# Five reordered operations at the seam of two sweeps in a hybrid encoder layer: a copy of masked scores, two low parts, one load and one gate

## The chip, the core and the metric

The kernel runs on one core of a Trainium2 chip. Its engines work side by side, each through its own queue in order: TensorE (PE, matrix products and transposes), VectorE (DVE), ScalarE (ACT), GpSimd (POOL), and SyncE (SP), which here only issues transfers. An instruction starts when those ahead of it on its engine have started and the semaphores it waits for have been raised; whatever stands behind a waiting instruction waits too. The metric is the device time of one execution in microseconds (us), as the median of several runs.

## What is computed

One encoder layer over 2048 tokens of width 1024: a gated linear attention in 4 heads (chunked, forward and backward scans) beside a latent attention in 4 heads (low-rank queries and keys/values, a shared rotary key, dense softmax), both gated, joined, projected and normalised.

```python
h = x @ w_in
(g_q, g_k, g_v, g_gate, g_lr_f, g_lr_b, m_cq, m_ckv, m_kr, m_gate) = jnp.split(h, idx, axis=-1)
# group A, per chunk and direction:
attn = jnp.where(mask, einsum('nbhtd,nbhsd->nbhts', q_dec, k_dec), 0.0)
o = einsum('nbhts,nbhsv->nbhtv', attn, vc) + einsum('bhtd,bhdv->bhtv', qd, state)
o_a = rms_norm(o_fwd + o_bwd, norm_g) * silu(g_gate)
# group B:
q = rms_norm(c_q, q_norm_g) @ w_uq
kv = rms_norm(c_kv, kv_norm_g) @ w_ukv
s = q_nope @ k_nope.T + rope(q_rope) @ rope(k_rope).T
o_b = softmax(s) @ v * silu(m_gate)
x = layer_norm(ALPHA * x + concat(o_a, o_b) @ w_out, ln_g, ln_b)
```

## The kernel before

**Precision.** Matrix operands in fp32 are carried as a high and a low part (`hi`, a copy into the matmul type, L378; `lo`, source minus high part, L384), and each product is three matmuls: high·high, high·low, low·high (`mm3`, L432 to L434). The high part is a copy on ACT; the low part is a subtraction on DVE or POOL.

**Stages.** There are 16 chunks of 128 tokens. The first sweep (`sweep_a`) goes through them from the last (15) to the first (0): input projections `ipa`, the gate product `ipg` and its silu (`gate_end`, tile `gs`, stored to `u_s`), the decayed queries and keys, the scores within a chunk `Ap`, the masked scores `At`, their product with the values `Op`, and the backward state. The gates of chunks 15 and 14 come behind it, with the loads and splits of the weights for what follows (`late_gates`). The second sweep (`sweep_c`) takes the chunks upwards, two to a step: projections `ipm` (448 columns: compressed queries `cq`, compressed keys/values `ckv`, the rotary key `kr`), gate products `pz`, the first group's output (`Ob`, then its norm and gate `og`), transposes `tm` of the compressed queries into `cqT` (high and low part), the rotary queries `pqr` and the absorbed queries `pq`. Then the softmax attention, with the output projection at its end.

**What sets the order.** In the second sweep a table of numbers sets it: every operation has a place per chunk of the pair, and all operations of all steps are sorted by step plus place; that is the order on each engine. The first step has a table of its own, `PLACE_C_FIRST`; its second entry is that of the odd chunk, chunk 1. The step's setup, `su_lset`, issues seven loads of small weights on SP. In the first sweep's last piece the code is in plain order, and `self.after(...)` around `gate_end(0, ...)` keeps the gate's instructions behind the named ones on the engines these run on.

**Names for the steps below.** In the last chunk of the first sweep, chunk 0, `At` is written twice: ACT copies half of `Ap` (L1071, PSUM to SBUF), then DVE overwrites it under a mask (L1073); PE needs it for `Op` (L1080). The gate of chunk 0 is three ACT passes over `gs` (L1582, L1584, L1586) and one product on DVE (L1588). In the second sweep `krf` (L1571) begins the rotary key on DVE, POOL completes it (L1400), ACT takes the high part `krs` and POOL the low part (L384, `krs<-krf,krs`). There is one `krf` buffer, so the next chunk's `krf` waits for that low part. `cqT_l` (L384 on DVE) is the low part of the compressed queries, which the third product of `pqr` reads (L434). `pq` takes the PSUM buffer that `Ob` of chunk 2 held, which is free when DVE has written `og` (L1554).

Of the kernel before, what the change touches and what calls it, by code (L numbers as in the profile page):

```python
# [12 lines left out]
AF = mybir.ActivationFunctionType  # L13
# [123 lines left out]
    cqTl=(0.758, 1.185),  # L137
# [51 lines left out]
    cqTl=(0.758, 1.284),  # L189
# [8 lines left out]
    krsl=(0.456, 1.044),  # L198
# [64 lines left out]
    ssm=(0.095, 0.913),  # L263
    rmd=(0.194, 0.9775),
    krf=(-0.407, 0.869),
    cqTl=(0.579, 1.316),
    ckvTl=(0.54, 1.33),
    qrf=(0.9795, 1.46),
    qrTl=(1.322, 1.703),
# [2 lines left out]
    Sf1=(-1.303, -0.0225),  # L272
    Sf2=(-0.613, -0.022),
    krfa=(-0.119, 0.94),
    krsl=(0.252, 1.09),
    vl=(0.627, 1.365),
    qrfa=(1.04, 1.476),
    lS=(-1.12, -1.093),
# [48 lines left out]
    cqTl=(0.598, 1.211),  # L327
# [8 lines left out]
    krsl=(0.395, 0.879),  # L336
# [30 lines left out]
class K:  # L367
# [272 lines left out]
    def sweep_a(self):  # L640
        tc, nc, ins, cp = self.tc, self.nc, self.ins, self.cp
        with ExitStack() as ctx:
# [61 lines left out]
            ch = self.ch = [dict(cst, c=NCH - 1 - i, i=i, lr=lrs[i % 2]) for i in range(NCH)]  # L704
# [48 lines left out]
            for t in ORDER_A.split():  # L753
                n, i = t.split(".")
# [22 lines left out]
            i = NCH - 1  # L777
# [6 lines left out]
                    run("kt", i)  # L784
            self.xlate.append(self.split_x(self.xab, self.xraw, NCH - 2, "xb", "dve", 2))
            run("intra", i)
            with self.after(ch[i]["Aset"]):
                self.gate_end(0, g1)
            run("state", i)
            run("av", i)  # L790
# [271 lines left out]
    def ga_intra(self, d):  # L1062

        nc, c = self.nc, d["c"]
        Ap = d["gp"].tile([P, 2, H, P], F32, tag="gp", name=f"Ap{c}")
        for h in range(H):
            for j, r in enumerate((slice(0, 64), slice(64, 128))):
                nc.tensor.matmul(Ap[:, j, h], d["kd"][r, h], d["qd"][r, h], start=True, stop=True)
        yield
        At = d["At"] = self.t512(d, "At")  # L1070
        nc.scalar.activation(At, Ap[:, 1], AF.Copy)  # L1071
        yield
        d["Aset"] = nc.vector.copy_predicated(At, d["mask"][:, None, :].to_broadcast([P, H, P]), Ap[:, 0]).ins  # L1073
        yield
# [139 lines left out]
    def su_lset(self):  # L1214
        nc, ins, w1 = self.nc, self.ins, self.w1
        self.gq = self.bc.tile([P, 2], F32, name="gq")
        self.gkv_b = w1.tile([P, H, P], F32, tag="oT", name="gkv_b", bufs=2)[:, 0]
        t1 = w1.tile([P, 2, 512], F32, tag="qa", name="wkr")
        self.wkT = t1[:, 0].rearrange("p (h l) -> p h l", h=H)
        self.wqr = t1[:, 1].rearrange("p (c d) -> p c d", c=2)  # L1220
        self.wqT = w1.tile([P, H, 256], F32, tag="gm", name="wqT")
        for t, n in ((self.gq, "gq_col"), (self.gkv_b, "gkv_bc"), (self.wqr, "wqr"), (self.wkT, "wkT"),
                     (self.wqT, "wqT"), (self.gkv_c, "gkv_col"), (self.gn_c, "gn_col")):
            nc.sync.dma_start(t, ins[n])
        self.wa = [None, None]

# [935 lines left out]
```

## Time and profile before

| | us |
|---|---|
| median of three runs (lowest, highest) | 1252.93 (1252.37, 1253.10) |
| the profiled execution, its own time | 1252.8 |
| its span, first to last instruction | 1251.0 |
| PE busy in the span | 1232.6 |
| DVE, ACT, POOL busy | 908.6, 732.1, 729.6 |
| mean granted TensorE clock | 0.999 |

The span is 1.8 us shorter than the execution's time, which also holds what lies around the instructions. PE is busy 99% of the span by modelled ends of pipelined matmuls, so what can be gained without removing work is the 18 us in which PE stands still, and these lie in few places. In a row of the timeline below stand the start, the duration, the engine, the line, the operation with output and inputs and their shapes, and in brackets how long the engine had stood idle before it and what released it.

### The profile page before, as it was taken

How to read it: one execution, taken by the hardware profiler on the slowest of the kernel's cores; microseconds unless marked ns; L12 is line 12 of the kernel's file. 1: busy time of each engine (PE TensorE's matmuls, PEld its weight loads, DVE VectorE, ACT ScalarE, POOL GpSimd, SP SyncE). 2: the span in 40 equal slices, each digit the busy share in tenths (PEclk: the TensorE clock that was granted, in tenths of full speed). 3: DMA queues.
4: the chain of work that ended last, by engine and by line, in shares of the span. 5: the costliest groups of instructions: out<-in, count | busy, mean ns of one | idle time of the engine just before them, and what ended most of it. 6: DMA issues, size and time to landing. Idle time of an engine off the chain costs nothing.

```text
span 1251.0 us, 18895 instructions
## 1 busy us (share of the span) xinstructions
PE 1232.6 (99%) x6464; PEld 1066.4 (85%) x6464; DVE 908.6 (73%) x1695; ACT 732.1 (59%) x1171; POOL 729.6 (58%) x445
## 2 busy tenths in 40 slices
PE   8999999999999999999999999999999999999997
PEld 7999999999888889897788888888888888888886
DVE  6636454544566776676999999899999998388775
ACT  7543434344565555545888888888888888411110
POOL 0132313232355555531798888889999999954650
PEclk9999999999999999999999999999999999999999
DMA  8225555555756888869543333313346310376652
GB/s 297 72 81 131 133 146 137 142 138 145 256 185 205 245 249 249 249 182 215 95 70 65 58 59 60 76 26 76 76 110 122 77 47 19 129 242 221 214 180 83
DMA packets 311568, 173.95 MB, mean 139 GB/s; under 512 B 212806, under 2 KB 264910, under 8 KB 311472
## 3 DMA queue, kind: packets, MB, share of 16 engines
q1 hardware_dynamic: 310352, 170.62, 50.9%
q0 software_dynamic: 672, 2.10, 0.4%
q8 instruction: 51, 0.84, 0.3%
q14 instruction: 45, 0.37, 0.1%
q10 hardware_dynamic: 448, 0.03, 0.0%
HBM read 113.93 MB, written 67.14 MB: 145 GB/s over the span
## 4 chain that ended last, share of the span: by engine, by line
PE 93%; ACT 2%; DVE 2%; DMA 2%; issue 1%; SPq 0%; POOL 0%; DVEq 0%; ACTq 0%; POOLq 0%
PE ipm L1366 5%; PE o L432 5%; PE o L434 5%; PE o L433 5%; PE ipa L432 5%; PE pS L1640 5%; PE pS L1636 5%; PE pS L1638 5%; PE pS L1637 5%; PE pS L1639 4%; PE ipa L434 4%; PE ipa L433 4%; PE po L433 3%; PE po L434 3%; PE po L432 3%; PE ipg L434 2%
## 5 line engine op out<-in xcount | busy, mean ns | idle before, releaser
L384 POOL TENSOR_TENSOR pl<-s,ph 128x1024 fp32r<-128x1024 f32 x128 | 306.9, 2417 | 47.6 <-ACT ph L378 43.9
L1645 ACT ACTIVATE s<-pS 128x1024 f32<-128x1024 f32 x128 | 131.5, 1028 | 54.8 <-PE pS L1640 49.8
L1658 DVE TENSOR_TENSOR rm<-pS,rm 128x512 f32<-128x512 f32 x210 | 144.7, 689 | 18.2 <-ACT s L1645 12.7
L1682 DVE TENSOR_TENSOR s<-s,mb 128x1024 f32<-128x1024 f32 x128 | 151.2, 1213 | 9.2 <-PE mb L1676 9.1
L378 ACT ACTIVATE ph<-s 128x1024 fp32r<-128x1024 f32 x128 | 134.9, 1056 | 15.6 <-PE o L434 15.0
L1686 ACT ACTIVATE s<-s 128x1024 f32<-128x1024 f32 x128 | 131.6, 1051 | 10.7 <-DVE s L1682 10.0
L432 PE MATMUL ipa<-wah,xah 128*128 128x384 f32 (+1 forms) x384 | 128.6, 335 | 5.0 <-ACT wah L378 5.0
L433 PE MATMUL ipa<-wal,xah 128*128 128x384 f32 (+1 forms) x384 | 124.4, 324 | 0.7 <-DVE wal L384 0.7
L434 PE MATMUL ipa<-wah,xal 128*128 128x384 f32 (+1 forms) x384 | 124.1, 323 | 0.0
L1105 POOL TENSOR_TENSOR Sb<-Sb,Us 64x512 f32<-64x512 f32 x15 | 19.9, 1325 | 170.2 <-DVE Us L1097 161.1
L1636 PE MATMUL pS<-qh,kvT 128*128 128x512 f32 x256 | 102.7, 401 | 0.8 <-DVE rm L1658 0.4
L432 PE MATMUL o<-ph,vh 128*128 128x512 f32 x256 | 101.1, 395 | 0.0
L1640 PE MATMUL pS<-rl,kvT 128*128 128x512 f32 x256 | 100.0, 391 | 0.6 <-DMA rl<-qr_s 0.6
L1638 PE MATMUL pS<-qh,kvT 128*128 128x512 f32 x256 | 100.0, 391 | 0.0
L1637 PE MATMUL pS<-ql,kvT 128*128 128x512 f32 x256 | 99.9, 390 | 0.0
L1639 PE MATMUL pS<-rh,kvT 128*128 128x512 f32 x256 | 99.8, 390 | 0.0
L434 PE MATMUL o<-ph,vl 128*128 128x512 f32 x256 | 99.7, 390 | 0.0
L433 PE MATMUL o<-pl,vh 128*128 128x512 f32 x256 | 99.7, 389 | 0.0
L1709 DVE TENSOR_TENSOR ap<-ap,s 128x512 f32<-128x512 f32 x120 | 82.9, 691 | 2.7 <-ACT s L1686 0.7
L432 PEld LDWEIGHTS ipa<-wah,xah 128*128 128x128 f32 x384 | 72.6, 189 | 8.3 <-ACT wah L378 5.4
L433 PEld LDWEIGHTS ipa<-wal,xah 128*128 128x128 f32 x384 | 72.8, 189 | 2.1 <-DVE wal L384 1.5
L1714 POOL TENSOR_TENSOR acc<-acc,s 128x1024 f32<-128x1024 f32 x30 | 72.6, 2420 | 1.1
(312 smaller groups left out, 3255.8 us busy)
## 6 DMA issues: line engine op xcount, KB each, us to landing
xcf<-xT_dram SPq DMA_DIRECT2D x16, 512.0 KB, 5.2
xr<-x_dram SPq DMA_DIRECT2D x16, 512.0 KB, 6.5
out_dram<-rr SPq DMA_DIRECT2D x32, 256.0 KB, 3.3
xaf<-xT_dram SPq DMA_DIRECT2D x14, 512.0 KB, 4.1
oib<-oi_s SPq DMA_DIRECT2D x16, 256.0 KB, 5.2
qdb<-qd_s SPq DMA_DIRECT2D x16, 256.0 KB, 3.3
SU<-su_s SPq DMA_DIRECT2D x16, 256.0 KB, 5.2
ub<-u_s SPq DMA_DIRECT2D x16, 256.0 KB, 4.0
```

What stands on the lines that cost most here:

```text
L378: return nc.scalar.activation(dst, src, AF.Copy).ins
L384: return e.tensor_tensor(dst, src, hi.bitcast(F32), ALU.subtract).ins
L432: mm(out, ah, bh, start=start, stop=False)
L433: mm(out, ah, bl, start=False, stop=False)
L434: mm(out, al, bh, start=False, stop=stop)
L1636: mm(ps[:, e], kh, qh, start=True, stop=False)
L1637: mm(ps[:, e], kh, ql, start=False, stop=False)
L1638: mm(ps[:, e], kl, qh, start=False, stop=False)
L1639: mm(ps[:, e], kr, rh, start=False, stop=False)
L1640: mm(ps[:, e], kr, rl, start=False, stop=True)
L1658: V.tensor_tensor(d["rm"], src[:, e], d["rm"], ALU.max)
L1682: V.tensor_tensor(s, s, d["mb"][:, None, :].to_broadcast([P, 2, QB]), ALU.subtract)
```

## The change

Four edits, no operation added or taken away. Two numbers of `PLACE_C_FIRST`, those of chunk 1: `cqTl` from 1.316 to 1.206 and `krsl` from 1.09 to 1.035. `gate_end(0, ...)` is kept behind the ACT copy of `At` too, and not only behind the masked overwrite on DVE. The load of `gkv_b` goes from second to last of the seven.

```diff
@@ PLACE_C_FIRST
-    cqTl=(0.579, 1.316),
+    cqTl=(0.579, 1.206),
-    krsl=(0.252, 1.09),
+    krsl=(0.252, 1.035),
@@ sweep_a
             run("intra", i)
-            with self.after(ch[i]["Aset"]):
+            with self.after(ch[i]["Acopy"], ch[i]["Aset"]):
                 self.gate_end(0, g1)
@@ ga_intra
-        nc.scalar.activation(At, Ap[:, 1], AF.Copy)
+        d["Acopy"] = nc.scalar.activation(At, Ap[:, 1], AF.Copy).ins
@@ su_lset
-        for t, n in ((self.gq, "gq_col"), (self.gkv_b, "gkv_bc"), (self.wqr, "wqr"), (self.wkT, "wkT"),
-                     (self.wqT, "wqT"), (self.gkv_c, "gkv_col"), (self.gn_c, "gn_col")):
+        for t, n in ((self.gq, "gq_col"), (self.wqr, "wqr"), (self.wkT, "wkT"), (self.wqT, "wqT"),
+                     (self.gkv_c, "gkv_col"), (self.gn_c, "gn_col"), (self.gkv_b, "gkv_bc")):
             nc.sync.dma_start(t, ins[n])
```

**First place: ACT at the end of the first sweep, before.** `xbh` is the high part of chunk 14's input, for its late gate, `gs` the gate of chunk 0, `At` the masked scores, `oi` the evacuation of `Op`.

```order
L378 ACTIVATE kt_3672<-kt_3667 128x512
L378 ACTIVATE xbh_3680<-xbf_3474 128x512 x2
L1582 ACTIVATE gs_3698<-ipg_3648 128x512
L1584 ACTIVATE gs_3698<-gs_3698 128x512
L1071 ACTIVATE At_3695<-Ap_3686 128x512
L1586 ACTIVATE gs_3698<-gs_3698 128x512
L1083 ACTIVATE oi_3720<-Op_3715 128x512
```

The same place of the changed kernel:

```order
L378 ACTIVATE kt_3672<-kt_3667 128x512
L378 ACTIVATE xbh_3680<-xbf_3474 128x512 x2
L1071 ACTIVATE At_3695<-Ap_3686 128x512
L1582 ACTIVATE gs_3698<-ipg_3648 128x512
L1584 ACTIVATE gs_3698<-gs_3698 128x512
L1586 ACTIVATE gs_3698<-gs_3698 128x512
L1083 ACTIVATE oi_3720<-Op_3715 128x512
```

The copy of `At` has moved past two of the gate's passes. With it the gate's product on DVE (L1588) goes behind the scaling of the state's update `Us` (L1097), and on POOL the store of `gs` goes behind those of `Us` and `oi`.

**Second place: DVE in the second sweep's first pair of chunks, where the rotary queries of chunk 0 are done, before.** `krf` and `rope` are the rotary key of chunk 2, `Ob` and `ss` the first group's output of chunk 2 and its norm, `cqT_l` the low part of chunk 1's queries.

```order
L1571 TENSOR_TENSOR krf_4283<-ipm_4188,cos 128x64
L1575 TENSOR_TENSOR rope_2_4284<-ipm_4188,sin 128x32 x2
L1534 TENSOR_TENSOR Ob_4271<-Ob_4271,oib_4096 128x512
L1421 STREAM_TRANSPOSE kvx_4289<-vh 128x128
L1421 STREAM_TRANSPOSE kvx_4289<-vl 128x128
L1421 STREAM_TRANSPOSE kvx_4289<-krs_4048 128x128
L1477 STREAM_TRANSPOSE qrx_4293<-qrf_4232 128x256
L1379 TENSOR_SCALAR ssm_4268<-ssm_4268 128x1 x2
L1543 TENSOR_REDUCE Ob_4271<-og_4305 128x4
L1544 TENSOR_SCALAR ss_4311<-Ob_4271 128x4
L384 TENSOR_TENSOR cqT_l_4102<-tm_4276,cqT_h_4101 128x2x128
L384 TENSOR_TENSOR qrT_4307<-qrx_4293,qrT_4307 128x256
```

DVE at the same place of the changed kernel:

```order
L384 TENSOR_TENSOR cqT_l_4102<-tm_4276,cqT_h_4101 128x2x128
L1571 TENSOR_TENSOR krf_4284<-ipm_4188,cos 128x64
L1575 TENSOR_TENSOR rope_2_4285<-ipm_4188,sin 128x32 x2
L1534 TENSOR_TENSOR Ob_4271<-Ob_4271,oib_4096 128x512
L1421 STREAM_TRANSPOSE kvx_4290<-vh 128x128
L1421 STREAM_TRANSPOSE kvx_4290<-vl 128x128
L1421 STREAM_TRANSPOSE kvx_4290<-krs_4048 128x128
L1477 STREAM_TRANSPOSE qrx_4294<-qrf_4232 128x256
L1379 TENSOR_SCALAR ssm_4268<-ssm_4268 128x1 x2
L1543 TENSOR_REDUCE Ob_4271<-og_4306 128x4
L1544 TENSOR_SCALAR ss_4312<-Ob_4271 128x4
L384 TENSOR_TENSOR qrT_4308<-qrx_4294,qrT_4308 128x256
```

`cqT_l` has moved past ten rows, to just ahead of `krf`.

**Third place: POOL beside it, before.** `krs` is the low part of chunk 1's rotary key, `qrf` the rotary queries of chunk 0, `xcl` the low part of chunk 3's input.

```order
L1400 TENSOR_TENSOR krf_4176<-krf_4176,rope_1_4177 128x64
L1473 TENSOR_TENSOR qrf_4232<-qrf_4232,rope_0_4233 128x256
L384 TENSOR_TENSOR krs_4243<-krf_4176,krs_4243 128x64
L384 TENSOR_TENSOR xcl<-xcf_4155,xch 128x8x128
L1511 TENSOR_TENSOR Sf_4280<-Sf_4071,cw 64x512
```

POOL at the same place of the changed kernel:

```order
L1400 TENSOR_TENSOR krf_4176<-krf_4176,rope_1_4177 128x64
L384 TENSOR_TENSOR krs_4243<-krf_4176,krs_4243 128x64
L1473 TENSOR_TENSOR qrf_4232<-qrf_4232,rope_0_4233 128x256
L384 TENSOR_TENSOR xcl<-xcf_4155,xch 128x8x128
L1511 TENSOR_TENSOR Sf_4280<-Sf_4071,cw 64x512
```

`krs` has moved past `qrf` and no longer stands behind what `qrf` waits for. On SP, `gkv_b` now follows `gn_c` and stands just ahead of the loads of the first group's stored states (`SU`); `gq` keeps its place and each of the other five loads moves up by one. PE's order is as it was.

## The prediction

> **What bounds the kernel now.** I read the page first for who sets the end, then the waits of PE, then the stretches by window, and last the timelines of all engines around each wait.
>
> ```profile
> span 1251.0 us, 18895 instructions
> PE 93%; ACT 2%; DVE 2%; DMA 2%; issue 1%; SPq 0%; POOL 0%; DVEq 0%; ACTq 0%; POOLq 0%
> PE pqr L434 <- DVE cqT_l L384: 1.1, 1, 1.1
> PE Op L1080 <- DVE At L1073: 0.6, 1, 0.6
> PE pq L432 <- DVE og L1554: 0.2, 1, 0.2
> 396.40:536.00 139.60, 139.60 (x780) 125.64 (x779) 97.33 (x333) 73.91 (x198) 77.52 (x82) 1.00 0.83 241
> ```
>
> The second line is the chain that ended last: 93% of it is PE. The next three are waits of PE between 325 and 410 us (total, times, longest). The last is a window (length, then busy time of PE, PEld, DVE, ACT, POOL, granted clock, DMA share, GB/s): PE is busy for all 139.60 us of the second sweep's middle. So PE sets the time, and an earlier start of that stretch moves everything behind it, as long as the helpers keep up. The edits bear on the three waits, which lie ahead of it.
>
> **First part: the copy of `At` ahead of the gate.**
>
> ```profile
> 332.83 1.16 PE L1068 MATMUL Ap<-qd,kd 64*128 64x128 f32 x16
> 335.15 0.40 PE L433 MATMUL ipg<-wgl,xbh 128*128 128x512 f32 x1
> 335.39 0.40 PE L434 MATMUL ipg<-wgh,xbl 128*128 128x512 f32 x1
> 336.36 1.16 PE L1080 MATMUL Op<-V,At 128*128 128x128 f32 x8 [0.58 <-DVE At L1073]
> 333.82 0.58 ACT L1582 ACTIVATE gs<-ipg 128x512 f32<-128x512 f32 x1
> 334.96 0.58 ACT L1071 ACTIVATE At<-Ap 128x512 f32<-128x512 f32 x1
> 333.42 1.29 DVE L384 TENSOR_TENSOR xbl<-xbf,xbh 128x512 fp32r<-128x512 f32 x2 [4.96 <-ACT xbh L378]
> 335.58 0.73 DVE L1073 COPY_PREDICATED At<-mask,Ap 128x512 f32<-128x512 int32 x1 [0.86 <-ACT At L1071]
> ```
>
> `Ap` ends at 332.83 + 1.16 = 333.99, and ACT is free for `At` from 333.82. So the copy starts at about 334.0 and ends at 334.6. DVE is busy with `xbl` until 333.42 + 1.29 = 334.71; the overwrite then runs from about 334.7 to 335.4, 0.9 us earlier. PE's product before `Op` starts at 335.39, and such products follow each other by 0.24 us (335.15 to 335.39), so `Op` could start at 335.63 and its operand is there by then. The gain is 336.36 − 335.63 = **0.73 us**; its floor is the listed idle time, 0.58, its ceiling the 0.9 by which `At` is earlier. What pays: the gate's passes end some 0.5 us later, at about 336.4, and the next ACT work (the evacuation of `Op`) can't start before `Op`'s new end, 336.8. That hides it; without this cover it would cost one pass, 0.58. The gate's product on DVE goes behind `Us`, and nobody but its store reads it soon.
>
> **Second part: the two low parts.**
>
> ```profile
> 380.65 0.47 DVE L1575 TENSOR_TENSOR rope<-pqr,sin 128x128 f32<-128x128 f32 x2
> 382.25 0.23 DVE L1571 TENSOR_TENSOR krf<-ipm,cos 128x64 f32<-128x64 f32 x1 [1.13 <-POOL krs L384]
> 385.01 0.41 DVE L384 TENSOR_TENSOR cqT_l<-tm,cqT_h 128x256 fp32r<-128x256 f32 x1
> 385.34 0.51 DVE L384 TENSOR_TENSOR qrT<-qrx,qrT 128x256 fp32r<-128x256 f32 x1
> 385.78 0.15 DVE L456 TENSOR_TENSOR rg_t<-Ob,ss 128x4 f32<-128x4 f32 x1
> 386.55 1.13 DVE L1554 SCALAR_TENSOR_TENSOR og<-Ob,rg_r,ub 128x128 f32<-128x128 f32 x4
> 381.20 0.74 POOL L1473 TENSOR_TENSOR qrf<-qrf,rope 128x256 f32<-128x256 f32 x1 [7.22 <-DVE rope L1575]
> 381.90 0.32 POOL L384 TENSOR_TENSOR krs<-krf,krs 128x64 fp32r<-128x64 f32 x1
> 382.18 2.40 POOL L384 TENSOR_TENSOR xcl<-xcf,xch 128x1024 fp32r<-128x1024 f32 x1
> 376.98 0.24 ACT L378 ACTIVATE krs<-krf 128x64 fp32r<-128x64 f32 x1
> 379.48 0.37 ACT L378 ACTIVATE cqT_h<-tm 128x256 fp32r<-128x256 f32 x1
> 385.37 0.18 ACT L446 ACTIVATE Ob<-rg_l 128x4 f32<-128x4 f32 x1
> 385.48 0.39 PE L434 MATMUL pqr<-wqr_h,cqT_l 128*128 128x256 f32 x1 [1.13 <-DVE cqT_l L384]
> 387.82 0.35 PE L432 MATMUL pq<-cqT_h,wabs_h 128*128 128x256 f32 x1 [0.19 <-DVE og L1554]
> ```
>
> Here DVE stands 1.13 us before `krf`, because POOL's `krs` is queued behind `qrf`, which itself waits 7.22 us for DVE's `rope`. ACT has the high part at 376.98 + 0.24 = 377.22, so moved ahead, `krs` fits into POOL's idle 7 us and is done by 377.6; without that cover it would cost its 0.32. DVE ends `rope` at 381.12. `cqT_l` comes next (its input is there at 379.48 + 0.37 = 379.85) and takes 385.34 − 385.01 = 0.33 from start to start, so `krf` starts at 381.45 in place of 382.25: 0.80 earlier. The same 0.33 falls away further down, ahead of `qrT`; but `rg_t` needs ACT's result, ready at 385.37 + 0.18 = 385.55 against a start of 385.78, so of it some 0.2 counts. `og` ends 1.0 earlier. PE alone would gain more: the wait before `pqr`'s third product (1.13) and that before `pq` (0.19), 1.32 together. But `pq` needs the buffer that `og` frees, so `og`'s **1.0 us** counts, and about 0.3 us of PE's stall moves from `pqr` to `pq`. Ceiling 1.32; floor 0.1, from the first rival. All times of this part shift along with the first part's gain, since its engines work off PE's results there.
>
> **Third part: the load.**
>
> ```profile
> SPq L1224 <- DMA u_s<-gs: 1.4, 1, 1.4
> 346.64 0.33 SPq L1224 DMA_DIRECT2D gn_c<-gn_col_dram  x1
> 347.45 0.80 SPq L1492 DMA_DIRECT2D SU<-su_s  x2
> gkv_b<-gkv_bc_dram SPq DMA_DIRECT2D x1, 64.0 KB, 4.0
> 337.40 0.57 POOL L916 DMA_DIRECT2D u_s<-gs  x1
> 353.95 0.52 POOL L1523 MEMSET SU<- 64x512 f32 x1
> 356.07 0.74 DVE L1255 SCALAR_TENSOR_TENSOR wabs<-pabs,gq,gkv_b 128x512 f32<-128x512 f32 x1
> 359.73 1.06 PE L1531 MATMUL Ob<-SU,qdb 128*128 128x128 f32 x8
> ```
>
> The first row is SP's own wait at `gkv_b`: its memory is free only when the store of `gs` has landed, 343.7, some 6.3 us after issue. The first part makes that store later: it is now behind two more issues of 0.57 each, so at about 338.5, and lands at about 344.8. At the end of the list `gkv_b`'s turn comes after `gn_c`, about 347.0, when the store is done. It lands 4.0 later, at 351, and `wabs` reads it at 356.07. The six loads ahead go earlier, `SU` hardly moves. I price this part at nothing; cover: 5 us for `wabs`, and for `SU` the time from the clearing's end (354.47) to `Ob` (359.73, then 359.0), 4.5 us.
>
> **Sum.** 0.73 + 1.0 = 1.73 us off the profiled execution's own 1252.8: 1251.07. The median of the runs lies 0.13 above that execution, so I predict **1251.2 us** for the median. 0.2% is 2.5 us, about what a measurement of this kernel can tell from no change; the forecast is 0.14% faster, within it.
>
> **Rivals.** *A port shared by DVE and POOL* takes the second part's gain back.
>
> ```profile
> L384 DVE TENSOR_TENSOR qrT<-qrx,qrT x16: 404/468/1300, 385.3 to 572.3; 128x256 fp32r<-128x256 f32 x16
> 420.32 1.30 DVE L384 TENSOR_TENSOR qrT<-qrx,qrT 128x256 fp32r<-128x256 f32 x1
> 420.31 1.03 POOL L1524 TENSOR_TENSOR SU<-Sf,cw 64x512 f32<-64x512 f32 x1
> 384.54 1.03 POOL L1511 TENSOR_TENSOR Sf<-Sf,cw 64x512 f32<-64x512 f32 x1
> ```
>
> The 16 subtractions for `qrT` last 404 ns at least and 1300 at most (min/median/max); the longest began beside a POOL product of 1.03 and ended 0.28 after it, as if it had stood until that was over. After the change POOL's `xcl` runs from about 381.9 to 384.3, and `qrT` comes up at about 384.2 (385.34 − 0.80 − 0.33). If it waits for `xcl` alone it ends by 384.6, ahead of the start of `rg_t` at 384.75, and nothing is lost. If POOL's next, `Sf`, gets in first, `qrT` stands until 385.3, `rg_t` starts at 385.7 and 0.1 is left: 1252.93 − 0.83 = 1252.1. Against it: at 385.34 the same subtraction met `Sf` (384.54 to 385.57) and still ended at 385.85, so it went in ahead of the POOL work behind. The Trainium skill, page "SBUF — State Buffer", section "Who interferes with whom", has this as a rule: a DVE instruction with two SBUF inputs contends with a GpSimd instruction that reads SBUF, and whichever begins first keeps the port for its whole length. The trace agrees (1.30 beside 1.03); by that rule either case above can come about, and the sum would be 1251.2 or 1252.1.
>
> *Nothing arrives.* PE starts earlier but meets a fixed transfer later. Against it: the busy window above, in which no wait could absorb 1.7 us; for it: loads late in the sweep are not shown to move with PE. It would give 1252.9.
>
> *Slower: the store of `gs` holds up SP.* `gkv_b` now stands just ahead of `SU`. If the store, issued 1.1 later and beside more loads, took 18 us in place of 6.3 and landed at 356.5, `SU` would go out at 356.8, 9.3 late; less the 4.5 of cover, `Ob` of chunk 0 is 4.8 late: 1252.9 − 1.7 + 4.8 = 1256.0. It costs from a store of 13 us on (landing at 351.6), loses to before from 15, and 0.2% from 17.5. Against it: one such row, at 6.3, and 2 us to spare at `gn_c`.
>
> **How the numbers follow.** The forecast has 0.64, its own range 1250.5 to 1251.8 (from ceilings of 0.9 and 1.32 to floors of 0.58 and some 0.6, if `og` gains only part). The port has 0.10, nothing arrives 0.04, the slow store 0.06, and another loss of over 0.2% 0.05, since four engines are shifted against each other and each meeting of them can cost. A gain past both ceilings, below 1250.4, has 0.11: the three waits above and their pipelined edges are all that the forecast counts, and one more stall that goes would do. So faster by over 0.2% 0.11, slower by over 0.2% 0.11, within 0.78. The range, 1250.1 to 1252.9, takes in the port, the case where nothing arrives and the nearer part of the larger gain; it leaves out the losses.
>
> **What would show it.** `Op` starts some 0.7 us earlier without idle time before it. `krs` follows ACT's high part on POOL; `krf` on DVE has no wait for POOL; `pqr` runs through; `pq` waits about 0.5 us for `og`, 1.7 earlier in all. The window from 394.7 has PE busy without a gap, and every later start is 1.7 earlier. A `qrT` of over 0.9 us there means the port; an SP wait at `gkv_b` that pushes `SU` past 350 means the slow store. I would be wrong if PE showed a new wait between `Op` and 410, or if the starts moved and the end didn't.

## The result, and the profile after

| | before | changed |
|---|---|---|
| median of 13 runs of each (lowest, highest), us | 1252.35 (1251.42, 1253.19) | 1249.72 (1248.74, 1250.96) |
| ratio of the two, 95% interval | | 0.998 [0.9971, 0.9988] |
| span of the profiled execution | 1251.0 | 1246.9 |

The change makes the kernel 2.6 us faster, with an interval from 1.5 to 3.6. The forecast was 1.73 us and 1251.2 for the median; the difference lies inside the interval, the median outside the range, below 1250.1. Here are the waits of PE in the changed kernel from 325 us on, in total, times and longest.

```profile
PE mb L1676 <- DVE mc L1669: 0.8, 1, 0.8
PE pq L432 <- DVE og L1554: 0.5, 1, 0.5
PE pz L432 <- DVE og L1554: 0.5, 1, 0.5
PE pS L1636 <- DVE rm L1658: 0.4, 1, 0.4
```

The waits at `Op` and `pqr` are gone, and the one at `pq` has grown from 0.2 to 0.5, as the prediction had it. A wait of before that the prediction did not use, PE's 0.6 for `rl` at the attention's first scores (`pS`, L1640), is missing too. To see where the time went, the start of one instruction is subtracted from that of another in each kernel. These are the timeline's rows for the last `Ap` of the first sweep, `Op`, the first `pabs` and the first `pq` of the changed kernel.

```profile
331.74 1.16 PE L1068 MATMUL Ap<-qd,kd 64*128 64x128 f32 x16
334.53 1.05 PE L1080 MATMUL Op<-V,At 128*128 128x128 f32 x8
350.51 1.95 PE L1248 MATMUL pabs<-wkr,wqT 128*128 128x128 f32 x16
384.72 0.36 PE L432 MATMUL pq<-cqT_h,wabs_h 128*128 128x256 f32 x1 [0.55 <-DVE og L1554]
```

From `Ap` to `pabs` are 18.77 us, from `pabs` to `pq` 34.21. Before, `pabs` began at 352.48, so it was 19.65 and 35.34. The two places gave **0.88 and 1.13 us, 2.01 together**. The stages of all profiles, each a difference of starts in one execution:

| stage, us | before, three profiles | changed, two profiles |
|---|---|---|
| span's start to first `Ap` | 37.65, 36.84, 37.66 | 36.58, 37.60 |
| last `Ap` to first `pabs` | 19.65, 19.63, 19.61 | 18.77, 18.76 |
| `pabs` to first `pq` | 35.34, 35.34, 35.35 | 34.21, 34.21 |
| `pq` to the second sweep's last `Ob` but one | 154.54, 154.54, 154.58 | 154.58, 154.54 |
| first scores to first maximum `mx` | 21.89, 21.23, 22.34 | 21.21, 21.47 |
| mid-attention, `pS` to the second `o` behind it | 0.70, 0.70, 0.70 | 0.46, 0.46 |

The second, third and fourth rows repeat to 0.05 us and carry the two gains on. The first and the fifth differ by up to 1.1 us between executions of the same kernel. The first pair of spans, 4.1 us apart, had luck in both: 1.07 at the start, where no edit lies, and 0.68 at the first scores.

The last row is **one more place, worth 0.24 us**, in the attention, where no edit lies either. DVE subtracts the row maxima `mb`, made by PE, from the scores `s` (L1682); later it makes `ofl`, the low part of an earlier output, and PE's next product `o` waits for that. Here are the rows of the kernel before, then of the changed one; PEld is the loading of PE's weights.

```profile
806.47 0.60 PE L1676 MATMUL mb<-ident,mc 128*128 128x128 f32 x4
807.52 1.22 DVE L1682 TENSOR_TENSOR s<-s,mb 128x1024 f32<-128x1024 f32 x1 [0.92 <-PE mb L1676]
820.01 0.39 PE L1640 MATMUL pS<-rl,kvT 128*128 128x512 f32 x1
820.37 0.19 PEld L432 LDWEIGHTS o<-ph,vh 128*128 128x128 f32 x1 [0.40 <-DVE ofl L384]
820.37 0.50 PE L432 MATMUL o<-ph,vh 128*128 128x512 f32 x1
820.71 0.40 PE L433 MATMUL o<-pl,vh 128*128 128x512 f32 x1
```

```profile
802.69 0.60 PE L1676 MATMUL mb<-ident,mc 128*128 128x128 f32 x4
803.39 1.22 DVE L1682 TENSOR_TENSOR s<-s,mb 128x1024 f32<-128x1024 f32 x1 [0.57 <-PE mb L1676]
816.23 0.39 PE L1640 MATMUL pS<-rl,kvT 128*128 128x512 f32 x1
816.46 0.39 PE L432 MATMUL o<-ph,vh 128*128 128x512 f32 x1
816.69 0.39 PE L433 MATMUL o<-pl,vh 128*128 128x512 f32 x1
```

Before, DVE begins 0.45 us after `mb` has ended (806.47 + 0.60 = 807.07), in the changed kernel 0.10 after it. It then works almost without a break up to `ofl`, so `ofl` is late too, and the two steps from `pS` to the second `o` take 0.70 instead of 0.46. Every profile shows one of two values: about 0.70 in the three of before, in e1 and in e6, about 0.46 in the two of the change and in all the other experiments below. So it belongs to the kernel and not to the execution: either the load's move (e3, e11) or that of `cqT_l` (e10) is enough. What holds DVE there is not shown. With it the stages give 2.25 of the 2.63 us between the medians.

### The profile page after: what moved, and what is told of

It is laid out like the page before. It is cut to its first block, busy times and chain, and to the rows that moved or that the text cites. A ratio compares the mean times of both kernels' runs of the same rounds, so it can differ in the third digit from the quotient of the medians.

```text
span 1246.9 us, 18892 instructions
## 1 busy us (share of the span) xinstructions
PE 1230.8 (99%) x6464; PEld 1066.5 (86%) x6464; DVE 908.7 (73%) x1695; ACT 732.1 (59%) x1171; POOL 729.0 (58%) x445
## 4 chain that ended last, share of the span: by engine, by line
PE 94%; DVE 2%; ACT 1%; DMA 1%; issue 0%; SPq 0%; DVEq 0%; ACTq 0%
PE ipm L1366 5%; PE o L432 5%; PE o L434 5%; PE o L433 5%; PE ipa L432 5%; PE pS L1636 5%; PE pS L1640 5%; PE pS L1638 5%; PE pS L1637 5%; PE pS L1639 5%; PE ipa L434 4%; PE ipa L433 4%; PE po L432 3%; PE po L433 3%; PE po L434 3%; PE ipg L434 2%
## 5 line engine op out<-in xcount | busy, mean ns | idle before, releaser
L1682 DVE TENSOR_TENSOR s<-s,mb 128x1024 f32<-128x1024 f32 x128 | 151.2, 1212 | 8.9 <-PE mb L1676 8.8
L1640 PE MATMUL pS<-rl,kvT 128*128 128x512 f32 x256 | 100.0, 391 | 0.0
L384 POOL TENSOR_TENSOR ol<-of,oh 128x512 fp32r<-128x512 f32 x32 | 42.9, 1340 | 52.4 <-ACT oh L378 52.4
```

Of the source, the lines that this page charges most:

```text
L384: return e.tensor_tensor(dst, src, hi.bitcast(F32), ALU.subtract).ins
L1640: mm(ps[:, e], kr, rl, start=False, stop=True)
L1682: V.tensor_tensor(s, s, d["mb"][:, None, :].to_broadcast([P, 2, QB]), ALU.subtract)
```

## The experiments

Every run was timed with the kernel before on the same chip (11 runs of it against 33 of before, whose median was 1252.24 for e1 to e4, 1252.35 for e5 to e8, 1252.59 for e9 to e12). An interval is about 1.1 us to either side, so single waits are told apart by the stages, not by the times.

**e1, the scores alone.**

```diff
-            with self.after(ch[i]["Aset"]):
+            with self.after(ch[i]["Acopy"], ch[i]["Aset"]):
```

> Only the copy of the masked scores goes ahead of the gate. Two waits (theory: the change is worth what PE's two stalls were, 0.87 us at Op and 1.09 at pq, and the rest of the 2.6 us is chance of the single executions): from the last Ap to the first pabs 0.8 to 0.9 us shorter than before (19.65 before, 18.77 after the whole change), pq's lead over pabs as before (35.34), time 0.9 us less. Late wait (rival: an earlier start also frees the wait for the rl transfer at the attention's first scores, 0.6): that wait is gone here too, time 1.5 less. Load (rival: the moved load carries part of it): as two waits, and the late wait stays.

Measured: 1253.17 us, ratio 1.0004 [0.9995, 1.0012]. `Op` starts 0.74 earlier after `Ap`, but `Ap` to `pabs` takes 19.70, as before. Here are SP's own wait, its load of `gkv_b`, POOL's issue of the gate's store and PE's `pabs`.

```profile
SPq L1224 <- DMA u_s<-gs: 4.0, 1, 4.0
345.28 0.33 SPq L1224 DMA_DIRECT2D gkv_b<-gkv_bc_dram  x1
346.61 0.43 SPq L1224 DMA_DIRECT2D wqT<-wqT_dram  x1
338.26 0.55 POOL L916 DMA_DIRECT2D u_s<-gs  x1
352.45 1.80 PE L1248 MATMUL pabs<-wkr,wqT 128*128 128x128 f32 x14 [0.78 <-DMA wqT<-wqT_dram]
```

SP waits 4.0 us for the store at `gkv_b` (1.4 before). The store is issued at 338.26 and not at 337.40, and takes 6.9 us to land instead of 6.2. `wqT`, behind `gkv_b`, goes out at 346.61 (345.07 before) and lands in 5.7 us (5.1 before), and PE waits 0.78 us for it. None of the three theories had this: the scores' gain is lost again 16 us later. The new theory, "queue": the load must move for the scores' gain to get through. The wait for `rl` was there (0.5).

**e2, the two low parts alone.**

```diff
-    cqTl=(0.579, 1.316),
+    cqTl=(0.579, 1.206),
-    krsl=(0.252, 1.09),
+    krsl=(0.252, 1.035),
```

> Only the two low parts move. Two waits: from the first pabs to the first pq 1.0 to 1.1 us shorter than before (35.34 before, 34.21 after the whole change), the last Ap to pabs as before (19.65), time 1.1 us less. Late wait: the wait for rl is gone here too, time 1.7 less. Load: the wait for rl stays at about 0.6.

Measured: 1250.98 us, ratio 0.9988 [0.9979, 0.9997]; `Ap` to `pabs` 19.65, `pabs` to `pq` 34.26: 1.08 shorter. The wait for `rl` stayed (0.7). "Two waits" holds for this place.

**e3 and e11, the load alone, twice** (`gkv_b` last, as in the change's diff).

> Only the load of gkv_b goes last. Two waits: no PE stage changes by more than 0.1 us, time the same within its interval; the wait for rl is there or not by chance. Late wait: the wait for rl stays at 0.6, since PE is no earlier. Load: SU goes out some 0.7 us earlier, the wait for rl is gone, time 0.6 or more less.

> The load alone once more. Stages only (theory: the load alone changes no PE stage; its 0.4 us were chance): last Ap to pabs 19.6, pabs to pq 35.3; the wait for rl at the attention's start anywhere from 0 to 0.8; time the same. Late wait by the load (rival: with the load last the wait for rl is gone or small, 0 to 0.2 in the four profiles so far, against 0 to 0.8 in the six others): 0 to 0.2 again, time 0.4 less again.

Measured: 1251.86 us, ratio 0.9996 [0.9987, 1.0005], and 1251.71, ratio 0.9995 [0.9986, 1.0003]. `Ap` to `pabs` 19.61 and 19.65, `pabs` to `pq` 35.30 in both: the load alone shortens neither place. The wait for `rl` was missing in e3 and 0.5 in e11, so "late wait by the load", as it was put, is wrong. Both times lie some 0.4 to 0.9 us under before, and each interval holds no change. One stage is shorter in both: the place in the attention, 0.46 against 0.70. That 0.24 was in none of the theories.

**e4 and e12, the kernel before, again.**

> The kernel before once more, for a second profile. Two waits: the stalls at Op (0.58), pqr (1.1) and pq (0.2) again to 0.05 us; the start up to the first sweep and the wait for rl may differ by half a us or more. Late wait and load: the wait for rl again at 0.5 to 0.7. Time the same.

> The kernel before a third time. Stages only: last Ap to pabs 19.6, pabs to pq 35.3, the wait for rl anywhere from 0 to 0.8, start to the first scores 36.6 to 37.7. Late wait by the load: the wait for rl at 0.5 or more. Time the same.

Measured: 1252.18 and 1252.29 us, ratios 1.0001 [0.9992, 1.001] and 0.9999 [0.999, 1.0008]. The waits of PE in e12:

```profile
PE pqr L434 <- DVE cqT_l L384: 1.1, 1, 1.1
PE pS L1640 <- DMA rl<-qr_s: 1.1, 1, 1.1
PE Op L1080 <- DVE At L1073: 0.6, 1, 0.6
PE pq L432 <- DVE og L1554: 0.2, 1, 0.2
```

The three that the edits bear on repeat; the one for `rl` was 0.6 in the first profile of this kernel, absent in e4 and 1.1 here. It is a matter of the single execution.

**e5, the change without its load edit.**

> The change without its load edit. Queue (theory now: the later store of the gate holds gkv_b, and with it the weights behind it on SP, so that the scores' gain is lost at pabs unless the load moves): PE waits 0.7 to 0.9 us for wqT before pabs, last Ap to pabs 19.6 to 19.8 as before, pabs to pq 34.2; time 1.1 us less than before, 0.9 more than the whole change. Chance (rival: that wait in the run with the scores alone was one slow transfer): last Ap to pabs 18.8, no wait for wqT, time 2.0 less.

Measured: 1251.27 us, ratio 0.9987 [0.9978, 0.9996].

```profile
344.98 0.33 SPq L1224 DMA_DIRECT2D gkv_b<-gkv_bc_dram  x1
353.01 2.02 PE L1248 MATMUL pabs<-wkr,wqT 128*128 128x128 f32 x16 [1.60 <-DMA wqT<-wqT_dram]
```

PE waits 1.60 us for `wqT`, and `Ap` to `pabs` takes 20.54, 0.9 more than before and twice the stall that was expected: the store of `gs` had landed late again (SP waited 4.2), and `wqT` itself took 6.6 us against 5.1 before. The price is there each time and depends on two transfers. "Queue" holds, "chance" falls.

**e9, scores and load, without the low parts.**

> The scores' copy and the load together, without the two low parts. Queue (theory: the load is what lets the scores' gain through): no wait for wqT before pabs, last Ap to pabs 18.8 where the scores alone had 19.7 and the scores with the low parts 20.5; pabs to pq 35.3 as before; time 0.9 us less than before. Chance (rival: those waits for wqT were slow transfers): the two runs with the early load were unlucky, and this one shows 18.8 too but e1 and e5 can't then be told from it by their times.

Measured: 1251.17 us, ratio 0.9988 [0.9979, 0.9996]; no wait at `pabs`, `Ap` to `pabs` 18.76, `pabs` to `pq` 35.29. Against e1 only the load differs: 0.94 us in the stage, and the intervals of the ratios don't reach each other's middle. Without the load edit the copy of the scores gains nothing, with it 0.88.

**e6, the rotary key's low part alone; e10, the queries' low part alone** (one line each of e2's diff).

> Only the rotary key's low part moves on POOL. Chain (theory: pq is set by DVE's chain to og, which stood behind that low part): krf starts at rope's end, pabs to pq 34.1 to 34.2, that is 1.1 to 1.2 us shorter than before, with PE's wait at pqr down from 1.1 to 0.1 or less; time 1.1 to 1.2 less. Queries (rival: pqr's wait for cqT_l has to go first): the wait at pqr stays over 0.5, pabs to pq 34.7 or more.

> Only the queries' low part moves on DVE. Chain: krf still waits for POOL's low part of the rotary key (about 0.8 us, the rest of the 1.13 being filled by the moved subtraction), pqr runs through, and PE's stall moves to pq (1.0 or more there), pabs to pq 35.1, 0.2 us shorter than before; time the same within its interval. Queries (rival: pqr's stall is the cost): pabs to pq 34.2 to 34.4, time 1.0 less.

Measured: e6 1250.95 us, ratio 0.9987 [0.9978, 0.9996], `pabs` to `pq` 34.08; e10 1252.33, ratio 0.9998 [0.9989, 1.0007], `pabs` to `pq` 35.36. First e6, then e10:

```profile
380.48 0.21 DVE L1571 TENSOR_TENSOR krf<-ipm,cos 128x64 f32<-128x64 f32 x1
383.22 0.41 DVE L384 TENSOR_TENSOR cqT_l<-tm,cqT_h 128x256 fp32r<-128x256 f32 x1
386.00 0.36 PE L432 MATMUL pq<-cqT_h,wabs_h 128*128 128x256 f32 x1 [0.19 <-DVE og L1554]
```

```profile
381.85 0.23 DVE L1571 TENSOR_TENSOR krf<-ipm,cos 128x64 f32<-128x64 f32 x1 [0.80 <-POOL krs L384]
384.61 0.86 DVE L384 TENSOR_TENSOR qrT<-qrx,qrT 128x256 fp32r<-128x256 f32 x1
387.44 0.36 PE L432 MATMUL pq<-cqT_h,wabs_h 128*128 128x256 f32 x1 [1.65 <-DVE og L1554]
384.14 1.04 POOL L1511 TENSOR_TENSOR Sf<-Sf,cw 64x512 f32<-64x512 f32 x1
```

In e6 `krf` follows `rope` at once, and 1.26 us are gained without touching `cqT_l`; with the rotary key out of the way it comes in time by itself. In e10 PE's wait at `pqr` is gone as well, and nothing is gained up to `pq`: PE waits 1.65 there instead. So DVE's chain to `og` set the time and the wait at `pqr` was only where PE happened to stand. e10 also misses the 0.2 that was expected: `qrT` began beside POOL's `Sf` and ended at 385.47, 0.29 after it (384.14 + 1.04 = 385.18), at 0.86 against 0.51 before. That fits the port of the first rival, met in another kernel.

**e7, the change without the move of `cqT_l`.**

> The change without the move of cqT_l. Chain: last Ap to pabs 18.8, pabs to pq 34.1 to 34.2, time 2.0 to 2.1 us less than before, the same as the whole change or 0.1 better. Queries: pabs to pq 34.7 or more, time 1.4 less.

Measured: 1249.86 us, ratio 0.9979 [0.997, 0.9988]; `Ap` to `pabs` 18.78, `pabs` to `pq` 34.02. From `pabs` to `pq` it is 0.19 us shorter than the change, with one edit less; by the times the two can't be told apart.

**e8, the change again.**

> The changed kernel once more. Stages only (theory: 0.88 at Op and 1.13 at pq are all that the change brings, and the rest of the first difference is chance): last Ap to pabs 18.8, pabs to pq 34.2; the start and the wait for rl differ from the first profile; time 2.0 us less than before, ratio 0.9984. More (rival: something else in the change is worth 0.6): ratio 0.9979 again, and a third stage that is shorter in both profiles than in those of before.

Measured: 1250.32 us, ratio 0.998 [0.9972, 0.9989]; 18.76 and 34.21 in the stages again, the start 1.02 later than in the first profile, a wait of 0.2 for `rl`. The ratio came out as "more" had it, and so did a third stage: the place in the attention, 0.46 in both profiles of the change and 0.70 in all three of before. So "stages only", which had the two places bring everything, is wrong by that 0.24.

## Why the prediction was right in its places and wrong in its number

*What bounds the kernel.* Right: the two places moved PE's start. From `pq` to the last `Ob` but one of the sweep the time stayed at 154.5 to 154.6, and from there to the first scores at 28.5 to 28.8 in all five profiles, so what was gained got through. **The step that failed here** is that the three waits "and their pipelined edges are all that the forecast counts": a fourth stall, 0.24 in the attention, went too. The prediction named "one more stall that goes" as the way to a larger gain, but had no candidate, and the place was luck.

*First part, `At`, 0.73.* The mechanism is right, the term was too small: 0.88. `Op` starts 0.74 earlier after `Ap`, as priced; the rest comes behind its start, where the prediction had no term. These are ACT and DVE in the changed kernel, then PE's weight loads for `Op` before, then after:

```profile
332.95 0.60 ACT L1071 ACTIVATE At<-Ap 128x512 f32<-128x512 f32 x1
333.58 0.74 DVE L1073 COPY_PREDICATED At<-mask,Ap 128x512 f32<-128x512 int32 x1
```

```profile
336.36 0.97 PEld L1080 LDWEIGHTS Op<-V,At 128*128 128x128 f32 x8 [1.02 <-DVE At L1073]
```

```profile
334.37 1.03 PEld L1080 LDWEIGHTS Op<-V,At 128*128 128x128 f32 x8
```

`At` is the weight operand of `Op`. Before, its first load starts with the matmul, at 336.36; now it starts at 334.37, 0.16 ahead of the matmul at 334.53, while the product before still runs, and `Op` is shorter too (1.05 against 1.16). That the early load is why `Op` is shorter fits the rows, but no run shows it alone. The copy follows `Ap` directly and the overwrite follows the copy, as worked out.

*Second part, the low parts, 1.0.* Right in mechanism, 1.13 measured. DVE and POOL in the changed kernel:

```profile
378.63 0.47 DVE L1575 TENSOR_TENSOR rope<-pqr,sin 128x128 f32<-128x128 f32 x2
379.02 0.41 DVE L384 TENSOR_TENSOR cqT_l<-tm,cqT_h 128x256 fp32r<-128x256 f32 x1
379.35 0.21 DVE L1571 TENSOR_TENSOR krf<-ipm,cos 128x64 f32<-128x64 f32 x1
382.09 0.46 DVE L384 TENSOR_TENSOR qrT<-qrx,qrT 128x256 fp32r<-128x256 f32 x1
375.28 0.32 POOL L384 TENSOR_TENSOR krs<-krf,krs 128x64 fp32r<-128x64 f32 x1 [3.28 <-ACT krs L378]
379.88 2.40 POOL L384 TENSOR_TENSOR xcl<-xcf,xch 128x1024 fp32r<-128x1024 f32 x1
382.23 1.22 POOL L1511 TENSOR_TENSOR Sf<-Sf,cw 64x512 f32<-64x512 f32 x1
```

`krs` runs in POOL's idle time, `krf` waits for nobody. The next instruction starts 0.39 after `rope`, not 0.47: the row's duration holds a tail that overlaps with what follows, which the prediction counted as full; that is 0.08 of the 0.13 too little. It did not price the two moves apart, and up to `pq` that of `cqT_l` gains nothing: it costs 0.18 (34.26 in e2 against 34.08 in e6) and 0.19 (the change against e7), since it stands ahead of `krf` on the chain that sets `pq`.

*The port.* As forecast, `qrT` came up beside `xcl` and got in ahead of `Sf`: it ended at 382.55, 0.27 after `xcl`, and `Sf` took 1.22 instead of 1.03. Nothing was lost, but it was close; e10 shows the same subtraction caught by `Sf`. By the Trainium skill's page "SBUF — State Buffer", section "Who interferes with whom", whichever of the two engines begins first keeps the port for its whole instruction; both cases agree with that.

*Third part, the load, priced at nothing.* At this seam the sum needed no term for it, but the reason was incomplete. The prediction saw that the store of `gs` would be later and that `gkv_b` in its new place would find it done. It did not ask what the old place would have cost then: 0.8 and 1.6 us of PE at `pabs` (e1, e5), as much as the first part brings or more. The load edit is what lets the 0.88 through. The rival of the slow store named this very queue, but looked at `SU` behind it and not at `wqT`.

*The number.* The forecast of the median missed by 1.48. **The step that weighed most** is "the median of the runs lies 0.13 above that execution, so I predict 1251.2": the three runs shown gave 1252.93, these and ten more of the same kernel 1252.35, so 0.58 of the miss was in the starting point, whose spread of executions (start and `rl`) the range didn't hold. The two terms were 2.01 and not 1.73, 0.28 too little, by the sizes above. The place in the attention is another 0.24. The rest, about 0.4, **stays open**; it may be chance, since 2.25 lies inside the interval of both measurements. The forecast's own range is also not the sum it is said to be: 1252.93 less the two ceilings, 0.9 and 1.32, is 1250.7 and not 1250.5.

*Nothing arrives* and *slower* did not come about; SP's `SU` went out at 345.7, before 350.

## What to carry to other kernels

A wait that PE shows names where it stands, not what to mend: undoing the wait at `pqr` alone moved it whole to `pq`, while freeing the helper's chain behind `pq` gained 1.26 us. When an edit makes a store later, look at every queue that waits for the memory it holds, and at all that stands behind that wait, in the order as it is without the other edits. And where the gain is a thousandth, take differences of starts within single stages, most of which repeat to 0.05 us, and a starting time from more than three runs. Compare the starts through the whole kernel, not only where the edits lie: a third of a microsecond of DVE's idle time, far behind them, went with either of two edits.

## What the runs showed that had not been expected

The same kernel's executions differ by 0.8 us before the first `Ap` (36.84 to 37.66) and by 1.1 us at the wait for `rl` (none to 1.1), while the stages between agree to a few hundredths. A product whose weights came late cost more than its matmul's listed idle time: 0.58 were listed, 0.88 were had back, with the weight load's own wait at 1.02. And an edit changed PE's time by 0.24 us more than 400 us behind itself, where the order on PE, DVE, ACT and POOL is the same in both kernels.
